# Layer 0 of a two-layer attention step: gates of heads 2 to 7 projected ahead of these heads' attention and applied with the norm; the sum of exponentials divided out in ScalarE's copy

## The chip, the core and the metric

The kernel runs on one core of one Trainium2 chip (trn2). The time is the device time of one execution in microseconds (us). In the rows of the profile PE is TensorE (PEld its weight loads), DVE is VectorE, ACT is ScalarE, POOL is GpSimd and SP is SyncE, which here only issues DMAs, in order. L694 is line 694 of the kernel before; in the changed kernel the same code stands a few lines further down.

## The reference, cut to what matters

Two layers over 1024 latent tokens and 256 context tokens of width 1024: layer 0 mixes by differential attention, layer 1 by multi-head latent attention. Each layer normalizes its input, shifts and scales it by a modulation computed from a conditioning vector, mixes, and adds the gated and normalized result. All values are fp32. Of layer 0, what bears on the change:

```python
q, k, v, gate = jnp.split(h @ w_in, ...)      # 8 heads; v and gate: 128 columns per head
def block(qb):
    s = jnp.einsum('bqhcd,bkhcd->bhcqk', qb, k) * scale
    p = jax.nn.softmax(s, axis=-1)
    w = p[:, :, 0] - lam * p[:, :, 1]
    return jnp.einsum('bhqk,bkhe->bqhe', w, v)
o = map_query_blocks(block, q)
o = rmsnorm(o, g_sub) * (1.0 - lam_init)      # over a head's 128 columns
return o.reshape(b, sq, MIX_WIDTH) * jax.nn.silu(gate)
```

The modulation is `silu(cond) @ w_ada + b_ada`, 3072 columns for each of the two layers.

## The kernel before

Tokens are held as five pairs of 128-token tiles: pairs 0 to 3 are the latent tokens, pair 4 (`CTXP`) the context. Large products are made of three matmuls each, high and low parts of both operands (`mm3`, L325 to L327).

Layer 0 runs from the start to about 965 us. A prologue ends near 60 us; then keys and queries are projected (list `P1`), to about 330 us; from there `l0_heads` runs 72 units, nine for each of the 8 heads (two for each latent pair, one for the context pair, pair order 0, 1, 4, 2, 3). Between the steps of a unit `feed(w)` advances a second stream of work by a share of the stream's estimated total. That stream is the list `P2`, whose items are joined by `chain`, which loads an item's weights while the item ahead still runs:

- `v1` to `v3` project the values, and `g0` to `g3` (in the list before: `g0` to `g2` and `y3`) the gates, of two heads each (hp = 0 to 3) for all five pairs. A pair's gate is evicted from PSUM by ACT (L487) and DVE (L488), which make twice its silu, and stored to the DRAM buffers `gdram` of the pair (L489; the trace's `g<-s`).
- `a0` to `a5` are modulation items (`ada_item`): each loads 8 pieces of `w_ada` of 128x512 fp32, 256 KB each, through the rings `wh` and `wl` of 5 buffers (L197), multiplies them (L188) with a 32-column tile, four of them writing to four different 32-row strips of one PSUM tile, copies the result out (L208) and turns it into columns (L233). Items `a6` and `a7` (`YA`) follow the last gate item.
- the last item, `gate_y_item`, projects one more pair of heads' gates, then runs `a6` and `a7`, and meanwhile steps through the list `gs` of `y_chunk(pr, kk)`; kk = 0 to 3 stands for heads 2kk and 2kk + 1. `YS` gives the counts of the stream at which a chunk may take its next step. A `y_chunk` loads 128x2x256 of the attention's result and of the gate (L750), into tiles named `kl`, `wst` or `xt`, multiplies them (DVE, L753), transposes the product by four (PE, L764), and writes the high part (ACT, L765) and the low part (DVE, L766) as operands of the out-projection. The chunks with kk = 3 are issued by `l0_heads` in the last head, and two of them after the attention (tiles `xt`).

A unit with an odd index, or of the context pair, ends with `l0_values`: the value matmuls, a copy of their sum (L688), two transposes (L691), a copy to `y` (L694). Its second half, called at the next unit's end, squares `y` times the reciprocal sum of exponentials `rz` with an accumulated sum (L698), makes the reciprocal root (DVE L250, POOL L252), multiplies by both on DVE (L702) and stores the head's 128 columns to `ydram` (L704, SP). There are 40 such posts, 5 for each head.

The PSUM tiles named `pj` come from one pool of 4 buffers, which the projections, the middle part of the scores, the transposes and the values share. The tiles `s` come from the pool `stg` with 4 buffers. SP issues every load and store named here in program order; a load that waits for a store or for a buffer holds up all behind it. The order on each engine is made by the scheduler of the language, from the program order and its own estimates.

After the attention come the out-projection of layer 0 and layer 1, to 1961 us. The change doesn't touch them.

Of the kernel before, what the change touches and what calls it, by code (L numbers as in the profile page):

```python
# [11 lines left out]
AF = mybir.ActivationFunctionType  # L12
ALU = mybir.AluOpType
# [68 lines left out]
class K:  # L82
    P1 = "k0 q0 k1 q1 k2 q2 k3 q3"
    P2 = "v1 a0 a1 v2 g0 a2 v3 a3 g1 a4 a5 g2 y3"
    YA = (6, 7)
# [589 lines left out]
    def l0_values(self, u, rz, vh, vl, feed):  # L675
# [4 lines left out]
        nch = 10 if lat else 2  # L680
        pv = self.t(c.tp, [P, 512], "pj")
        for ch in range(nch):
            g, j = ch // 4, ch % 4
            vs = ch if lat else 10 + ch
            self.mm3(pv[:, 0:256], (vh[:, vs, :], vl[:, vs, :]), (u.pth[g][:, j, :], u.ptl[g][:, j, :]),
                     ch == 0, ch == nch - 1)
# [6 lines left out]
        ss = self.t(c.st, [P, 2], "oss")  # L693
        nc.scalar.copy(y, pv[:, 256:512].rearrange("p (t d) -> p t d", t=2))  # L694
        yield

        for i in range(2):
            nc.scalar.activation(oT[:, i * P:(i + 1) * P], y[:, i, :], AF.Square,  # L698
                                 scale=rz[i], accum_out=ss[:, i:i + 1])
        r = self.rstd(c.st, ss, P, 2, tag="ors")  # L700
        for i in range(2):
            nc.vector.tensor_scalar(out=y[:, i, :], in0=y[:, i, :], scalar1=r[:, i:i + 1], scalar2=rz[i],  # L702
                                    op0=ALU.mult, op1=ALU.mult)
        nc.sync.dma_start(self.ydram[pr].rearrange("(t p) n -> p t n", p=P)[:, :, h * P:(h + 1) * P], y)  # L704
# [34 lines left out]
    def y_chunk(self, pr, kk, late=None, alt=False):  # L739

        nc, c = self.nc, self.c
        if late:
            y, g = (self.t(late, [P, 2, 256], "xt", bufs=3) for j in range(2))
        elif alt:
            y, g = (self.t(self.wp, [P, 2, 256], "wst", bufs=3) for j in range(2))
        else:
            yg = self.t(c.kst, [P, 2, 2, 256], "kl", bufs=4)
            y, g = yg[:, 0], yg[:, 1]
        for o, src in ((y, self.ydram), (g, self.gdram)):
            nc.sync.dma_start(o, src[pr].rearrange("(t p) n -> p t n", p=P)[:, :, kk * 256:(kk + 1) * 256])  # L750
        yield 1

        nc.vector.tensor_tensor(out=y, in0=y, in1=g, op=ALU.mult)  # L753
        yield 1
# [15 lines left out]
    def gate_y_item(self, hp, more):  # L770
# [7 lines left out]
        def gen(ws):  # L778
            gs = [self.y_chunk(pr, kk, alt=(3 * pr + kk) % 2) for pr in range(NPAIR) for kk in range(3)]
            at = self.YS  # L780
# [965 lines left out]
```

## Time and profile before

| | |
|---|---|
| time, median of 3 runs | 1967.2 us (1964.93 to 1968.94) |
| the profiled execution, its time | 1963.3 us |
| its span from first to last instruction | 1961.5 us |
| mean granted TensorE clock | 0.996 |
| PE busy over the span | 96% |
| DVE, ACT, POOL busy over the span | 68%, 49%, 3% |
| attention of layer 0 with its stream of projections | about 330 to 965 us |

Durations and waits are read from the profiled execution, which is 3.9 us below the median of the runs. A row of a group gives the line, the engine, the operation, the tiles written and read, the shape, the count, then the busy time in us and the mean of one in ns, then the engine's idle time ahead of these instructions and what ended it. Rows of a stretch give its start and end, its length, and for each engine the busy time and the count of instructions, then the granted clock, the mean share in which the 16 DMA engines were busy, and GB/s.

### The profile page before, as it was taken

What the parts mean: (1) busy time and instruction counts of PE and PEld (TensorE: products, weight loads), DVE (VectorE), ACT (ScalarE), POOL (GpSimd) and SP (SyncE); (2) the same over time, 40 slices, a digit from 0 to 9 for tenths busy, and PEclk for the clock granted to TensorE, in tenths of its full rate; (3) what the DMA queues carried; (4) which work ended last, traced back from release to release, by engine and by line L of the source; (5) the groups of instructions that cost most, each with busy time, mean ns of one, the idle gap of its engine ahead of it and who ended that gap; (6) DMA issues with size and microseconds to landing.
All of it is one profiled execution on the core that took longest, in us unless ns stands there. A gap on an engine that the chain in (4) does not pass through costs nothing.

```text
span 1961.5 us, 35893 instructions
## 1 busy us (share of the span) xinstructions
PE 1892.0 (96%) x13468; PEld 1712.6 (87%) x13468; DVE 1330.3 (68%) x2983; ACT 964.3 (49%) x2409; POOL 59.5 (3%) x91
## 2 busy tenths in 40 slices
PE   7999999999999999998999999999999999998998
PEld 5888888789989887987799998889899999997998
DVE  4655457788888788899537644337777877778524
ACT  4422124567666666776446633334444545456421
POOL 0000000000000000000000100000000000000000
PEclk9999999999999999999999999999999999999999
DMA  8555544444455554455525303441111111113512
GB/s 312 191 182 181 175 146 151 147 135 129 135 157 153 143 165 142 129 161 173 193 95 164 104 25 100 141 144 30 43 37 30 40 48 45 39 35 98 170 49 108
DMA packets 225006, 237.63 MB, mean 121 GB/s; under 512 B 25313, under 2 KB 192577, under 8 KB 224705
## 3 DMA queue, kind: packets, MB, share of 16 engines
q1 hardware_dynamic: 224672, 235.29, 38.7%
q8 instruction: 107, 1.75, 0.4%
q14 instruction: 67, 0.54, 0.1%
q10 hardware_dynamic: 160, 0.05, 0.0%
HBM read 160.48 MB, written 74.78 MB: 120 GB/s over the span
## 4 chain that ended last, share of the span: by engine, by line
PE 79%; DVE 11%; DMA 3%; ACT 3%; issue 2%; POOL 1%; SPq 0%; POOLq 0%; ACTq 0%; DVEq 0%
PE pj L325 16%; PE pj L327 16%; PE pj L326 16%; PE S L600 5%; PE tp L668 3%; PE tp L325 3%; PE tp L326 3%; PE tp L327 3%; DVE mA L602 2%; PE pj L668 2%; DVE ptl L671 2%; PE S L1274 1%; PE S L1276 1%; PE S L1277 1%; PE S L1275 1%
## 5 line engine op out<-in xcount | busy, mean ns | idle before, releaser
L325 PE MATMUL pj<-wh,hh 128*128 128x256 f32 (+1 forms) x1264 | 367.1, 290 | 9.1 <-DVE ptl L671 6.3
L326 PE MATMUL pj<-wl,hh 128*128 128x256 f32 (+1 forms) x1264 | 356.4, 282 | 2.3 <-DVE wl L318 2.3
L327 PE MATMUL pj<-wh,hl 128*128 128x256 f32 (+1 forms) x1264 | 356.2, 282 | 0.2
L325 PEld LDWEIGHTS pj<-wh,hh 128*128 128x128 f32 x1264 | 239.7, 190 | 14.4 <-DVE ptl L671 6.3
L326 PEld LDWEIGHTS pj<-wl,hh 128*128 128x128 f32 x1264 | 239.9, 190 | 3.5 <-DVE wl L318 2.9
L327 PEld LDWEIGHTS pj<-wh,hl 128*128 128x128 f32 x1264 | 239.4, 189 | 2.1 <-DVE hl L298 1.4
L325 PE MATMUL pj<-hh,wh 128*128 128x512 f32 (+1 forms) x512 | 188.6, 368 | 0.0
L327 PE MATMUL pj<-hh,wl 128*128 128x512 f32 (+1 forms) x512 | 188.1, 367 | 0.0
L326 PE MATMUL pj<-hl,wh 128*128 128x512 f32 (+1 forms) x512 | 188.0, 367 | 0.0
L614 ACT ACTIVATE e<-S,bias 128x1024 f32<-128x1024 f32 x128 | 143.0, 1117 | 80.9 <-DVE bias L611 80.6
L602 DVE TENSOR_REDUCE mA<-S 128x1 f32<-128x1024 f32 x128 | 155.4, 1218 | 25.4 <-PE S L600 24.9
L600 PE MATMUL S<-kl,q 128*128 128x512 f32 x512 | 148.6, 409 | 4.2 <-ACT e L614 3.6
L670 ACT CAST pth<-tp 128x512 fp32r<-128x512 f32 (+1 forms) x208 | 98.3, 511 | 79.0 <-PE tp L668 77.8
L670 ACT CAST pth<-pj 128x512 fp32r<-128x512 f32 (+1 forms) x192 | 98.0, 517 | 68.9 <-PE pj L668 66.0
L671 DVE TENSOR_TENSOR ptl<-tp,pth 128x512 fp32r<-128x512 f32 (+1 forms) x208 | 115.3, 582 | 12.3 <-ACT pth L670 11.5
L645 DVE SCALAR_TENSOR_TENSOR e<-e,cf,e 128x512 f32<-128x512 f32 (+1 forms) x192 | 117.6, 658 | 0.8
L671 DVE TENSOR_TENSOR ptl<-pj,pth 128x512 fp32r<-128x512 f32 (+1 forms) x192 | 113.2, 593 | 2.9 <-ACT pth L670 2.6
L318 DVE TENSOR_TENSOR wl<-wst,wh 128x512 fp32r<-128x512 f32 (+3 forms) x136 | 84.2, 629 | 41.2 <-ACT wh L317 40.4
L327 PEld LDWEIGHTS pj<-hh,wl 128*128 128x128 f32 x512 | 96.4, 188 | 17.2
L326 PEld LDWEIGHTS pj<-hl,wh 128*128 128x128 f32 x512 | 96.4, 188 | 16.8
L325 PEld LDWEIGHTS pj<-hh,wh 128*128 128x128 f32 x512 | 96.4, 188 | 16.8
L1291 ACT ACTIVATE e<-S,bias 128x1024 f32<-128x1024 f32 x64 | 71.5, 1118 | 76.4 <-DVE bias L1289 69.9
(316 smaller groups left out, 4941.4 us busy)
## 6 DMA issues: line engine op xcount, KB each, us to landing
q<-qsd SPq DMA_DIRECT2D x320, 64.0 KB, 2.0
wst<-in_da_w_in_dram SPq DMA_DIRECT2D x64, 256.0 KB, 3.1
kl<-ksd SPq DMA_DIRECT2D x64, 192.0 KB, 3.9
wst<-in_w_out_dram SPq DMA_DIRECT2D x48, 256.0 KB, 3.0
ast<-in_w_ada_dram SPq DMA_DIRECT2D x8, 1024.0 KB, 6.2
wh<-in_w_ada_dram SPq DMA_DIRECT2D x32, 256.0 KB, 4.3
wl<-in_w_ada_dram SPq DMA_DIRECT2D x32, 256.0 KB, 4.1
vdh<-s SPq DMA_DIRECT2D x24, 256.0 KB, 2.0
```

The lines of the kernel that those rows point to most:

```text
L318: nc.vector.tensor_tensor(out=wl, in0=st, in1=f32(wh), op=ALU.subtract)
L325: nc.tensor.matmul(out, a[0], b[0], start=first, stop=False)
L326: nc.tensor.matmul(out, a[0], b[1], start=False, stop=False)
L327: nc.tensor.matmul(out, a[1], b[0], start=False, stop=last)
L600: nc.tensor.matmul(S[:, so:so + 512], st(cc, o), kl[cc][:, so:so + 512], start=(o == 0), stop=(o == 1))
L602: nc.vector.reduce_max(out=mA[:, cc:cc + 1], in_=S, axis=AX.X)
L614: nc.scalar.activation(u.es[cc][:, 0:1024], A[cc], AF.Exp, bias=bias[:, cc:cc + 1], scale=0.125, accum_out=u.zA[:, cc:cc + 1])
L645: nc.vector.scalar_tensor_tensor(out=w[:, sl], in0=w[:, sl], scalar=cf, in1=e0[:, sl], op0=ALU.mult, op1=ALU.add)
L668: nc.tensor.transpose(tp[:, j, :], u.e[:, (c0 + j) * P:(c0 + j + 1) * P], self.ident)
L670: nc.scalar.copy(hi, tp[:, 0:cn, :])
L671: nc.vector.tensor_tensor(out=u.ptl[g][:, 0:cn, u.i * P:(u.i + 1) * P], in0=tp[:, 0:cn, :], in1=f32(hi), op=ALU.subtract)
L1291: nc.scalar.activation(e[:, 0:nm], S, AF.Exp, bias=bias, scale=sc, accum_out=Z[:, 0:1])
```

## The change

1. The list of the stream. Before, the gates of heads 0 to 5 are projected between the value items, and those of heads 6 and 7 last; after, the gates of heads 2 to 7 come right behind the values of these heads, and those of heads 0 and 1 last. The modulation items `a1` to `a5` stand in a row (before: `a0 a1`, `a2`, `a3` and `a4 a5` apart).
2. `l0_values` loads, for heads 2 to 7, the head's gate (tile `s`, 128x2x128, 128 KB, on SP) and multiplies with it where it applied `rz` before: `scalar_tensor_tensor` in place of `tensor_scalar`. Heads 0 and 1 keep a `tensor_scalar`, with one scalar.
3. `rz` is applied earlier: one copy of 128x256 (L694) becomes two activations of 128x128 with a scale, and the square (L698) has no scale any more.
4. `y_chunk` loads and multiplies the gate for kk = 0 only. The chunks of a pair are taken in the order kk = 1, 2, 0 and not 0, 1, 2.

```diff
-    P2 = "v1 a0 a1 v2 g0 a2 v3 a3 g1 a4 a5 g2 y3"
+    P2 = "v1 g1 v2 g2 a0 v3 g3 a1 a2 a3 a4 a5 y0"
...
     def l0_values(self, u, rz, vh, vl, feed):
...
+        if h > 1:
+            gt = self.t(c.stg, [P, 2, P], "s")
+            nc.sync.dma_start(gt, self.gdram[pr].rearrange("(t p) n -> p t n", p=P)[:, :, h * P:(h + 1) * P])
...
-        nc.scalar.copy(y, pv[:, 256:512].rearrange("p (t d) -> p t d", t=2))
+        for i in range(2):
+            nc.scalar.activation(y[:, i, :], pv[:, 256 + i * P:256 + (i + 1) * P], AF.Copy, scale=rz[i])
         yield
...
             nc.scalar.activation(oT[:, i * P:(i + 1) * P], y[:, i, :], AF.Square,
-                                 scale=rz[i], accum_out=ss[:, i:i + 1])
+                                 accum_out=ss[:, i:i + 1])
         r = self.rstd(c.st, ss, P, 2, tag="ors")
         for i in range(2):
-            nc.vector.tensor_scalar(out=y[:, i, :], in0=y[:, i, :], scalar1=r[:, i:i + 1], scalar2=rz[i],
-                                    op0=ALU.mult, op1=ALU.mult)
+            if h > 1:
+                nc.vector.scalar_tensor_tensor(out=y[:, i, :], in0=y[:, i, :], scalar=r[:, i:i + 1], in1=gt[:, i, :],
+                                               op0=ALU.mult, op1=ALU.mult)
+            else:
+                nc.vector.tensor_scalar(out=y[:, i, :], in0=y[:, i, :], scalar1=r[:, i:i + 1], scalar2=None,
+                                        op0=ALU.mult)
...
     def y_chunk(self, pr, kk, late=None, alt=False):
...
-            y, g = (self.t(late, [P, 2, 256], "xt", bufs=3) for j in range(2))
+            y, g = self.t(late, [P, 2, 256], "xt", bufs=3), None
         elif alt:
-            y, g = (self.t(self.wp, [P, 2, 256], "wst", bufs=3) for j in range(2))
+            y = self.t(self.wp, [P, 2, 256], "wst", bufs=3)
+            g = None if kk else self.t(self.wp, [P, 2, 256], "wst", bufs=3)
...
-        for o, src in ((y, self.ydram), (g, self.gdram)):
+        for o, src in ((y, self.ydram), (g, self.gdram))[:1 if kk else 2]:
             nc.sync.dma_start(o, src[pr].rearrange("(t p) n -> p t n", p=P)[:, :, kk * 256:(kk + 1) * 256])
         yield 1
 
-        nc.vector.tensor_tensor(out=y, in0=y, in1=g, op=ALU.mult)
+        if kk == 0:
+            nc.vector.tensor_tensor(out=y, in0=y, in1=g, op=ALU.mult)
...
-            gs = [self.y_chunk(pr, kk, alt=(3 * pr + kk) % 2) for pr in range(NPAIR) for kk in range(3)]
+            gs = [self.y_chunk(pr, kk, alt=(3 * pr + (kk + 2) % 3) % 2) for pr in range(NPAIR) for kk in (1, 2, 0)]
```

Three places show how the order of the engines' instructions moves. The first is PE, where one modulation item ends and the next begins. The last two of an item's 8 products (L188) are followed by the four small matmuls into columns (L233), and the next item's first products follow. Before, in the pair `a4 a5`; L600 and L608 are scores, L668 transposes of the exponentials:

```order
L188 MATMUL pj_9055<-wh_8807,silc_239 32x512
L188 MATMUL pj_9055<-wl_8808,silc_239 32x512
L600 MATMUL S_9142<-kl_7926,q_8989 128x512 x4
L600 MATMUL S_9155<-kl_7927,q_8989 128x512 x4
L233 MATMUL pj_9099<-sel_242,s_9097 128x2 x4
L188 MATMUL pj_9106<-wh_9078,silc_239 32x512
L188 MATMUL pj_9106<-wl_9079,silc_239 32x512
L668 MATMUL pj_9148<-identr_227,e_8917 128x128 x4
L668 MATMUL pj_9161<-identr_227,e_8917 128x128 x2
L188 MATMUL pj_9106<-wh_9080,silc_239 32x512
```

And after, one of the four such places in the row `a1` to `a5`:

```order
L188 MATMUL pj_10176<-wh_10086,silc_239 32x512
L188 MATMUL pj_10176<-wl_10087,silc_239 32x512
L233 MATMUL pj_10220<-sel_242,s_10218 128x2 x4
L600 MATMUL S_10256<-kl_9011,q_10114 128x512
L600 MATMUL S_10269<-kl_9012,q_10114 128x512
L600 MATMUL S_10256<-kl_9011,q_10114 128x512 x3
L600 MATMUL S_10269<-kl_9012,q_10114 128x512 x3
L188 MATMUL pj_10226<-wh_10199,silc_239 32x512
L188 MATMUL pj_10226<-wl_10200,silc_239 32x512
L668 MATMUL pj_10262<-identr_227,e_10025 128x128 x4
```

One item's passage to the next looks alike in both; after, there are four of them with no projection between, and the products stand in groups of other sizes along the stream.

The second place is DVE near the end of the attention, in the last head, where the chunks' multiplies (L753) stand among the weighing (L636 to L645) and the low parts of the exponentials (L671). Before:

```order
L766 SCALAR_TENSOR_TENSOR hl_2376_11436<-pj_11742,gsub_314_1097,hh_2375_11435 128x2x256
L640 SCALAR_TENSOR_TENSOR cf_11730<-Z_11549,neglam_1086,rz_11728 128x1
L753 TENSOR_TENSOR kl_11787<-kl_11787 128x512
L645 SCALAR_TENSOR_TENSOR e_11605<-e_11605,cf_11730,e_11604 128x512 x2
L645 SCALAR_TENSOR_TENSOR e_11605<-e_11605,cf_11730,e_11604 128x256
L753 TENSOR_TENSOR wst_11737<-wst_11737,wst_11738 128x512
L636 TENSOR_TENSOR Z_11672<-Z_11672,zA_11674 128x2
L753 TENSOR_TENSOR kl_11814<-kl_11814 128x512
L638 RECIPROCAL rz_11851<-Z_11672 128x2
L753 TENSOR_TENSOR kl_11905<-kl_11905 128x512
L671 TENSOR_TENSOR ptl_2459_11794<-pj_11797,pth_2456_11791 128x4x128
```

After, in the same head (L763 is the multiply's line there, L776 that of the low parts):

```order
L645 SCALAR_TENSOR_TENSOR e_11679<-e_11679,cf_11803,e_11678 128x512 x2
L645 SCALAR_TENSOR_TENSOR e_11679<-e_11679,cf_11803,e_11678 128x256
L636 TENSOR_TENSOR Z_11745<-Z_11745,zA_11747 128x2
L638 RECIPROCAL rz_11921<-Z_11745 128x2
L640 SCALAR_TENSOR_TENSOR cf_11923<-Z_11745,neglam_1086,rz_11921 128x1
L645 SCALAR_TENSOR_TENSOR e_11790<-e_11790,cf_11923,e_11789 128x512 x2
L671 TENSOR_TENSOR ptl_2483_11865<-pj_11868,pth_2480_11862 128x4x128
L645 SCALAR_TENSOR_TENSOR e_11790<-e_11790,cf_11923,e_11789 128x256
L671 TENSOR_TENSOR ptl_2484_11866<-pj_11877,pth_2481_11863 128x4x128
L763 TENSOR_TENSOR kl_11885<-kl_11885 128x512
L776 SCALAR_TENSOR_TENSOR hl_2490_11889<-pj_11890,gsub_314_1097,hh_2489_11888 128x512
```

Four multiplies stood in eleven rows; one is left, that of a chunk with kk = 0.

The third place is SP at the same stage: the loads of the chunks (L750, after: L759), the store of a fresh gate (L489), of a head's result (L704, after: L712) and the loads of `a6` and `a7` (L197). The names `y_5` and `g_10` are the context pair's `ydram` and `gdram`, `y_2` and `g_7` pair 1's. Before:

```order
L750 DMA wst_11737<-y_5_64 128x2x256
L750 DMA kl_11787<-y_1_60 128x2x256
L750 DMA kl_11787<-g_6_65 128x2x256
L197 DMA wh_11833<-in_w_ada_dram 128x512
L704 DMA y_5_64<-y_11538 128x2x128
L750 DMA wst_11738<-g_10_69 128x2x256
L197 DMA wl_11834<-in_w_ada_dram 128x512
L750 DMA kl_11814<-y_5_64 128x2x256
L750 DMA kl_11814<-g_10_69 128x2x256
L750 DMA kl_11905<-y_2_61 128x2x256
L750 DMA kl_11905<-g_7_66 128x2x256
L489 DMA g_10_69<-s_11704 128x2x256
```

After:

```order
L712 DMA y_5_64<-y_11612 128x2x128
L759 DMA kl_11885<-y_5_64 128x2x256
L759 DMA kl_11975<-y_2_61 128x2x256
L489 DMA g_10_69<-s_11777 128x2x256
L197 DMA wh_11905<-in_w_ada_dram 128x512
L197 DMA wl_11906<-in_w_ada_dram 128x512
L197 DMA wh_11907<-in_w_ada_dram 128x512
L759 DMA kl_11885<-g_10_69 128x2x256
L197 DMA wl_11908<-in_w_ada_dram 128x512
L197 DMA wh_11909<-in_w_ada_dram 128x512
```

The chunks' gate loads are gone but for kk = 0, and that of the last pair stands behind the store of the gate that it reads, with three loads of `w_ada` between.

## The prediction

> **What bounds the kernel now.** I read the page first: the head, the busy times and the shares of the chain of waits.
>
> ```profile
> span 1961.5 us, 35893 instructions
> PE 1892.0 (96%) x13468; PEld 1712.6 (87%) x13468; DVE 1330.3 (68%) x2983; ACT 964.3 (49%) x2409; POOL 59.5 (3%) x91
> PE 79%; DVE 11%; DMA 3%; ACT 3%; issue 2%; POOL 1%; SPq 0%; POOLq 0%; ACTq 0%; DVEq 0%
> ```
>
> PE is the bound. What an edit elsewhere can give back is PE's idle time, so I read next where that lies: the busy times by stretch, from the attention's body through its end to the out-projection.
>
> ```profile
> core 0: us, PE busy (x) PEld busy (x) DVE busy (x) ACT busy (x) POOL busy (x), PEclk, DMA share, GB/s
> 500.00:860.00 360.00, 353.95 (x2599) 317.10 (x2598) 309.24 (x675) 239.72 (x635) 18.47 (x23) 1.00 0.50 145
> 875.00:945.00 70.00, 61.90 (x441) 51.93 (x444) 66.67 (x143) 47.41 (x119) 4.18 (x5) 0.98 0.64 203
> 945.00:975.00 30.00, 26.74 (x217) 23.88 (x210) 13.56 (x27) 11.04 (x30) 0.69 (x1) 0.98 0.53 167
> ```
>
> In the body PE idles 6.05 of 360 us, which is 1.2 in 70, and DVE has 14% to spare. From 875 to 945 PE idles 8.1 of 70 us, and DVE is busy for 95%: there DVE is the bound. From 945 to 975, where the late chunks stand, PE idles 3.3. These three numbers are all that the attention has to give, unless PE's own work shrinks.
>
> **The chunks' multiplies.** L753 by stretch, its kinds, and the waits of that end:
>
> ```profile
> 836.00:865.00 29.00, 2.77 (x4) 1.00 0.48 140
> 865.00:960.00 95.00, 9.38 (x14) 0.98 0.57 177
> 960.00:975.00 15.00, 1.39 (x2) 1.00 0.74 237
> L753 DVE TENSOR_TENSOR xt<-xt,xt x2: 693/693/693, 967.9 to 971.9; 128x512 f32<-128x512 f32 x2
> DVE xt L753 <- DMA xt<-g: 3.9, 2, 2.8
> PE pj L764 <- DVE xt L753: 1.5, 1, 1.5
> ```
>
> Of 20 multiplies 5 stay. By the changed order of DVE 4 of them lie where 14 lay (865 to 960): 10 x 0.67 = 6.7 us less on an engine with 3.3 us free in 70. Each us that DVE is ahead there should come back to PE until PE's idle time falls to the body's 1.2, so at most 8.1 - 1.2 = 6.9. The lower end is 2: the engine still has the weighing and the low parts in a row, and PE's waits in that end are single ones of 1 to 1.5 us on different DVE results. I take **-5**, nearest to the amount of work taken off, less the part that falls between waits.
>
> The two late chunks (`xt`) lose multiply and gate load. Both sit in the out-projection's first stretch; DVE waits 3.9 us for the two gate loads and PE 1.5 for DVE. The load of `y` remains on the path, so I take only PE's own wait, **-1.5**, between 0 and the whole 3.3.
>
> **The modulation items.** L188 alone, by the stretches of the eight items, 16 records each:
>
> ```profile
> 373.00:377.00 4.00, 1.92 (x16) 0.42 (x16) 1.00 0.84 267
> 377.00:389.00 12.00, 6.29 (x16) 0.84 (x16) 1.00 0.61 194
> sum 63.00, PE 30.59 PEld 4.77; mean PE 3.82 PEld 0.60
> ```
>
> The same 8 products cost 1.92 us in one run and 6.29 in six pieces: up to four that follow each other run side by side on their strips, and a lone one takes as long as four. In the order before, the eight items fall into 2, 6, 4, 4, 2, 6, 3 and 2 such pieces, 29, so 30.59 / 29 = 1.05 us each. After, they are 2, 2, 5, 2, 4, 4, 3 and 4: 26. That is 3 x 1.05 = **-3.1** on PE itself; ends -2 and -4, as PE's order may fill such gaps otherwise.
>
> Five items stand in a row now, and they bring 40 loads of 256 KB with little projection between. What loads at full rate did to PE before:
>
> ```profile
> 376.00:382.00 6.00, 5.84 (x28) 2.93 (x26) 3.76 (x11) 3.62 (x10) 0.69 (x1) 1.00 1.00 322
> 736.00:752.00 16.00, 15.61 (x85) 7.75 (x83) 12.63 (x26) 7.95 (x23) 0.69 (x1) 1.00 0.66 206
> 924.00:938.00 14.00, 12.03 (x79) 8.23 (x80) 13.94 (x30) 8.99 (x24) 0.13 (x1) 1.00 1.00 339
> SPq L197 <- PE pj L327: 20.4, 14, 4.2
> ```
>
> In the pairs `a0 a1` (376) and `a4 a5` (736) PE lost 0.16 of 6 and 0.4 of 16 us, so the lower end is 0. One item's 2.1 MB at 322 GB/s takes 6.5 us. In the new order some 21 us of other PE work stands between the five, 5.2 for each of four gaps, so each gap could lack 1.3 us; with 3 more for the other 3.3 MB that SP moves there (10 us at that rate, most of it in the row's own 26 us), the upper end is +8. I take **+2**: nearer to the pairs, which had the same load ahead by one item, and rings of the same depth.
>
> **The copy and the square.** The rows of ACT that price the split, and who waits for the copy:
>
> ```profile
> L694 ACT COPY y<-pj 128x256 f32<-128x256 f32 x40 | 15.0, 376 | 13.3 <-PE pj L691 11.2 <-DMA y<-y 1.2 <-DVE Z L636 0.4
> L418 ACT COPY r<-pj 128x512 f32<-128x512 f32 x32 | 18.8, 586 | 130.5 <-PE pj L327 130.4
> L765 ACT ACTIVATE hh<-pj,gsub 128x512 fp32r<-128x512 f32 x20 | 13.7, 694 | 16.0 <-PE pj L764 16.0
> L698 ACT ACTIVATE oT<-y,rz 128x128 f32<-128x128 f32 x64 | 25.4, 400 | 0.6
> L1034 ACT ACTIVATE rjunk<-qa 128x384 bf16<-128x384 f32 x10 | 5.3, 526 | 0.2
>   PE pj L188: 1.5, 1
> ```
>
> Copies cost 0.82 ns a column (586 - 376 over 256), so 271 for 128; a scale from memory adds 694 - 586 = 108. Two activations make 758 against 376, +382 ns. A square without a scale of that kind, from L1034 less 256 columns, is 316 against 400, and a post has two: -168. Net 0.21 us a post, 8.6 over 40. The cover is ACT's spare time, 33% in the body and 22.6 of 70 us at the end. What is not covered is the release of the `pj` tile, 0.38 later in each post: PE waited for L694 by 1.5 us once. I take **+1**; ends 0 and 1.9, five posts' delay in the last head, where everything is late already. With the end's DVE loosened, ACT is what would be late next.
>
> **The gate within the post.** `scalar_tensor_tensor` with the gate takes the place of `tensor_scalar`, 60 times:
>
> ```profile
> L702 DVE TENSOR_SCALAR y<-y,ors,rz x64: 336/343/350, 348.8 to 958.7; 128x128 f32<-128x128 f32 x64
> L645 DVE SCALAR_TENSOR_TENSOR e<-e,cf,e 128x512 f32<-128x512 f32 x128 | 91.7, 747 | 0.8
> L632 DVE SCALAR_TENSOR_TENSOR e<-e,cfx 128x256 f32<-128x256 f32 x16 | 7.3, 480 | 0.1
> ```
>
> The operation takes 747 ns at 512 and 480 at 256, 1.04 a column, so 346 at 128 against 343: **0**. The most is 0.9 us in the last stretch, were each 70 ns dearer; below zero nothing speaks for it.
>
> The Trainium skill speaks against this edit: "VectorE: DVE Perf Modes", section "The perf-mode tier table (the rule you actually need)", gives fp32 `tensor_scalar` in SBUF twice the rate, and an operation with two tensor inputs the single one. By it 128 columns would take some 67 ns more (an estimate from that page's durations), 4 us over the 60, of them 0.9 in the last stretch, and the sum below would be -4.7. The trace doesn't bear it out: by the rows of L645 and L632 the two cost the same at this size.
>
> The 30 loads of 128 KB that fetch the gate stand on SP:
>
> ```profile
> y<-y SPq DMA_DIRECT2D x40, 128.0 KB, 1.9
> wst<-g SPq DMA_DIRECT2D x7, 256.0 KB, 4.3
> g<-s SPq DMA_DIRECT2D x20, 256.0 KB, 2.2
> ```
>
> They are issued ahead of the value matmuls and needed after the norm, some 10 us of work later, so a 4.3 us load is covered in the body: **0**. The 15 gate loads of the chunks that go are 3.9 MB, and so are the 30 added, so traffic is level. The upper end is +3: in head 6 the load of a post stands behind 16 loads of `w_ada`, and late gates hold the single `y` buffer, whose store had the copy wait 1.2 us in the row of L694.
>
> Chunks with kk = 0 load a gate that was just projected. For the last pair, 2.2 us for the store and 4.3 for the load make 6.5, beside some 8.7 us of other DVE work that the new order puts between, but with three loads of 256 KB ahead in the queue. **+1**, ends 0 and +4 (2 us for those three loads and 2 more if the store waits as well).
>
> **The sum.** -5 - 1.5 - 3.1 + 2 + 1 + 0 + 0 + 1 = -5.6 us, against the profiled execution's 1963.3: 1957.7. That execution lies 3.9 below the runs' median of 1967.2, so the forecast for the median is **1961.6**, 0.29% faster. About 0.2%, 3.9 us, is what a measurement of this kernel can tell from no change. With every low end the sum is -14, with every high one about +14.
>
> **Rivals.** *No change: the end is bound by more than DVE.* In 924 to 938 the DMA engines are full too (1.00, 339 GB/s, the loads of `a6`), and both stay. If the last posts' chain through SP and POOL and these loads set the pace, the DVE relief yields only 2, and the late chunks 0, since `y` of the last head must still be stored and loaded: -2 - 3.1 + 2 + 1 + 1 = -1.1, 1966.1. For it: the single waits there come from many sides. Against: DVE was busy 13.94 of those 14 us.
>
> *Slower: SP stands still in the row of five.* SP waits for a ring buffer with everything behind it, queries and gates included; before, that was 20.4 us in 14 waits, all hidden. If one batch of 16 loads, 4.2 MB, 12.7 us at 330 GB/s, delays a query load or a post's gate fully once, that is +12.7 in place of +2: -5.6 + 10.7 = +5.1, 1972.3. It decides from a stall of 11.5 us on, which moves the sum past +3.9. Against: the pairs before lost 0.4 us at most, and queries are loaded three units ahead.
>
> *A larger gain: all idle time at the end returns, and nothing is paid elsewhere:* -6.9 - 3.3 - 3.1 + 1 for the copy = -12.3, 1954.9. For it: 95% against the body's 86% on DVE.
>
> **How the numbers follow.** Forecast 0.47 (own range 1957 to 1965), no change 0.28, slower 0.14, the larger gain 0.11. Faster than 0.2% means 1963.3 or less: 0.38 of the forecast's chance, all of the larger gain and 0.05 of the no-change case, 0.54. Within: 0.09 + 0.20 + 0.03 of the slower case, 0.32. Slower: 0.03 + 0.11 = 0.14. The range 1951 to 1971 takes in both bounds of the forecast's large terms and leaves out the deep end of the stall and of the gain.
>
> **What the changed profile would show.** In the last 70 us of the attention DVE below 90% busy and PE's idle time near 3 us; in the next 30 no wait for a gate load; L188 near 27.5 us in all; the two activations near 380 ns and the multiply with the gate near 345; in the row of five, PE's idle time below 3 us, with DMA share near 1. The forecast is wrong if PE's idle time at the end stays at 8 with DVE relieved, if a wait for `w_ada`, a query or a gate of several us shows in head 6, or if PE's waits for the copies' tile grow past a few us.

## The result, and the profile after

The changed kernel takes 1992.8 us (median of four runs, 1990.9 to 1994.9) against 1966.9 for the kernel before: ratio 1.0129, 95% interval 1.0115 to 1.0143. It is 26 us slower, where 5.6 us less were forecast. The profiled execution took 1990.9. The head of its page, its busy times and the shares of its chain of waits:

```profile
span 1989.1 us, 35955 instructions
PE 1901.3 (96%) x13468; PEld 1719.0 (86%) x13468; DVE 1322.9 (67%) x2968; ACT 964.6 (48%) x2449; POOL 58.8 (3%) x91
PE 77%; DVE 13%; ACT 3%; DMA 3%; issue 2%; POOL 1%; SPq 0%; ACTq 0%; POOLq 0%; DVEq 0%
```

The span grew by 27.6 us. PE ran as many matmuls, was busy 9.3 us longer, and idled 87.8 us where it had idled 69.5, 18.3 more. Where the idle time came shows in the busy times by stage. From 500 us on the stages are cut at the same points of the work in both kernels: at the first scores of head 6, of head 7, at the last scores, and some 55 us later, in the out-projection. First before, then after:

```profile
core 0: us, PE busy (x) PEld busy (x) DVE busy (x) ACT busy (x) POOL busy (x), PEclk, DMA share, GB/s
330.00:500.00 170.00, 160.09 (x1158) 141.80 (x1157) 140.62 (x307) 109.12 (x285) 7.93 (x10) 1.00 0.47 137
500.00:780.00 280.00, 274.13 (x1996) 242.41 (x1995) 237.90 (x523) 184.30 (x487) 14.65 (x18) 1.00 0.51 148
780.00:854.00 74.00, 73.89 (x565) 69.66 (x563) 65.68 (x144) 50.60 (x134) 3.82 (x5) 1.00 0.51 144
854.00:927.00 73.00, 67.91 (x486) 60.31 (x487) 69.19 (x146) 53.24 (x139) 4.18 (x5) 1.00 0.50 149
927.00:980.00 53.00, 46.66 (x361) 39.46 (x360) 32.74 (x67) 24.96 (x62) 1.38 (x2) 0.97 0.63 206
```

```profile
330.00:500.00 170.00, 161.74 (x1210) 150.11 (x1210) 143.28 (x314) 112.37 (x305) 7.57 (x10) 1.00 0.41 118
500.00:771.00 271.00, 257.60 (x1920) 237.10 (x1919) 230.94 (x502) 180.72 (x496) 15.03 (x18) 1.00 0.49 140
771.00:869.00 98.00, 89.14 (x576) 66.40 (x575) 70.04 (x154) 50.87 (x140) 3.45 (x5) 0.97 0.63 189
869.00:945.00 76.00, 69.46 (x504) 62.37 (x504) 66.42 (x140) 52.61 (x141) 3.81 (x5) 1.00 0.53 158
945.00:1000.00 55.00, 46.67 (x310) 36.95 (x309) 25.81 (x54) 20.81 (x54) 1.38 (x2) 0.88 0.46 146
```

PE's idle time in the body (500 us to head 6) went from 5.9 to 13.4 us, in head 6 from 0.1 to 8.9, in head 7 from 5.1 to 6.5, behind it from 6.3 to 8.3; from 330 to 500 us it is 9.9 and 8.3. The body's 7.5 us are nearly as large a loss as head 6's 8.8, and no term of the prediction stands for them. Head 6, where the five modulation items now stand in a row, takes 98 us and not 74 (part of that is the items' own work, which left the heads ahead of it). In head 7 DVE is relieved as forecast, 87% busy and not 95%, and PE idles there no less than before: in this stage the relief bought nothing.

The other 9.3 us are the clock, the granted share of TensorE's full speed. These rows are stretches of the changed kernel; the number behind the busy times is the granted clock:

```profile
816.00:820.00 4.00, 2.20 (x18) 0.45 (x17) 3.25 (x13) 2.92 (x14) 0.69 (x1) 1.00 0.17 46
820.00:828.00 8.00, 6.38 (x20) 4.38 (x20) 4.90 (x10) 0.00 (x0) 0.00 (x0) 0.57 0.91 300
956.00:960.00 4.00, 2.12 (x19) 1.88 (x18) 2.88 (x6) 2.39 (x7) 0.69 (x1) 1.00 0.63 207
960.00:968.00 8.00, 6.54 (x28) 3.53 (x28) 4.21 (x11) 2.44 (x4) 0.00 (x0) 0.57 0.27 88
978.00:982.00 4.00, 0.94 (x7) 0.46 (x5) 2.17 (x5) 3.28 (x11) 0.69 (x1) 0.90 0.19 65
982.00:988.00 6.00, 5.92 (x27) 5.92 (x28) 0.02 (x1) 0.00 (x0) 0.00 (x0) 0.50 0.66 188
```

Behind three pauses of PE the clock stands at half for some 7 us: 0.43 x 8 twice, and 0.1 x 4 with 0.5 x 6, make 3.4 us lost in each of three places. The profiled execution of the kernel before has one such place in the attention, behind a wait of 1.5 us for the copy that two of the three pauses also wait for (below):

```profile
PE pj L233 <- DVE s L208: 1.5, 1, 1.5
942.00:944.00 2.00, 1.70 (x11) 1.73 (x12) 2.00 (x5) 0.00 (x0) 0.40 (x1) 0.72 0.41 136
944.00:948.00 4.00, 4.00 (x26) 1.52 (x25) 2.50 (x7) 1.91 (x4) 0.00 (x0) 0.71 0.22 64
```

0.28 x 2 and 0.29 x 4 make 1.7 us. Part of the difference is luck of the execution: this one had a mean clock of 0.996, where the middle one of 83 executions of the kernel before, beside the experiments, had 0.993. What PE waited for in the row of five, and in the end:

```profile
PE pj L233 <- DVE s L208: 3.2, 1, 3.2
PE pj L233 <- DVE m L610: 1.4, 1, 1.4
PE S L600 <- ACT e L614: 1.4, 1, 1.4
PE pj L188 <- DMA wh<-in_w_ada_dram: 1.3, 1, 1.3
PE pj L233 <- DVE s L208: 3.3, 1, 3.3
PE xt L923 <- ACT gp L928: 2.3, 1, 2.3
```

The first four rows are from 790 to 850 us, the last two from 945 to 1000. In both stages the longest is a modulation item's column step (L233) that waits for DVE's copy of its products out of PSUM (L208). In the body of the kernel before no such wait was over 0.6 us. The order of PE tells why. Where I showed it ahead of the prediction I called the passages alike in both kernels; they are not. Before, eight scores stand between an item's last products and its column step; after, in the place shown, the column step follows at once. In the traces 4 to 50 matmuls stand there in the kernel before; in the row of five it is 4, 10, 0, 2 and 0, and behind the two zeros PE stands idle for 3.2 and 1.4 us, while the copy is still behind other work on DVE.

In the end 18 matmuls stand there in both kernels, and the copy is later. DVE's only wait between 957 and 962 us, and the chain of waits (start, length, what):

```profile
DVE hl L776 <- ACT hh L775: 1.0, 2, 0.5
958.82 0.60 ACT hh L775
...
960.11 0.60 DVE y L707 x2
960.71 0.61 DVE s L208
...
961.46 1.84 PE pj L233 x8
```

The products are there at 956.0, and the copy starts at 960.6. Ahead of it in DVE's queue stand, among others, a chunk's multiply (L763), two chunks' low parts (L776), which wait 1.0 us for their high parts on ACT (L775), and a post's multiply with the gate (L707). PE stands at L233 until that is through, and starts again at half clock.

### The profile page after: what moved, and what is told of

The parts are those of the page before. It is cut to its first block, busy times and chain, and to the rows that moved or that the text cites. A ratio compares the mean times of both kernels' runs of the same rounds, so it can differ in the third digit from the quotient of the medians.

```text
span 1989.1 us, 35955 instructions
## 1 busy us (share of the span) xinstructions
PE 1901.3 (96%) x13468; PEld 1719.0 (86%) x13468; DVE 1322.9 (67%) x2968; ACT 964.6 (48%) x2449; POOL 58.8 (3%) x91
## 4 chain that ended last, share of the span: by engine, by line
PE 77%; DVE 13%; ACT 3%; DMA 3%; issue 2%; POOL 1%; SPq 0%; ACTq 0%; POOLq 0%; DVEq 0%
PE pj L325 16%; PE pj L327 15%; PE pj L326 15%; PE S L600 4%; PE tp L668 3%; DVE mA L602 3%; PE tp L325 3%; PE tp L326 3%; PE tp L327 3%; DVE ptl L671 2%; PE pj L668 2%; PE S L1286 1%; PE S L1287 1%; PE S L1284 1%; PE S L1285 1%
## 5 line engine op out<-in xcount | busy, mean ns | idle before, releaser
L614 ACT ACTIVATE e<-S,bias 128x1024 f32<-128x1024 f32 x128 | 143.0, 1117 | 94.2 <-DVE bias L611 94.2
L600 PE MATMUL S<-kl,q 128*128 128x512 f32 x512 | 149.4, 412 | 7.0 <-ACT e L614 7.0
L671 DVE TENSOR_TENSOR ptl<-tp,pth 128x512 fp32r<-128x512 f32 (+1 forms) x208 | 115.3, 582 | 12.3 <-ACT pth L670 11.5
L645 DVE SCALAR_TENSOR_TENSOR e<-e,cf,e 128x512 f32<-128x512 f32 (+1 forms) x192 | 118.8, 658 | 1.3
L671 DVE TENSOR_TENSOR ptl<-pj,pth 128x512 fp32r<-128x512 f32 (+1 forms) x192 | 113.3, 593 | 4.8 <-ACT pth L670 4.6
L317 ACT CAST wh<-wst 128x512 fp32r<-128x512 f32 (+3 forms) x136 | 77.1, 574 | 71.8 <-PE pj L326 21.0
L668 PE MATMUL pj<-identr,e 128*128 128x128 f32 x640 | 106.2, 275 | 5.0 <-DVE e L645 1.9
```

The costliest lines, as they stand in the source:

```text
L317: nc.scalar.copy(wh, st)
L600: nc.tensor.matmul(S[:, so:so + 512], st(cc, o), kl[cc][:, so:so + 512], start=(o == 0), stop=(o == 1))
L614: nc.scalar.activation(u.es[cc][:, 0:1024], A[cc], AF.Exp, bias=bias[:, cc:cc + 1], scale=0.125, accum_out=u.zA[:, cc:cc + 1])
L645: nc.vector.scalar_tensor_tensor(out=w[:, sl], in0=w[:, sl], scalar=cf, in1=e0[:, sl], op0=ALU.mult, op1=ALU.add)
L668: nc.tensor.transpose(tp[:, j, :], u.e[:, (c0 + j) * P:(c0 + j + 1) * P], self.ident)
L671: nc.vector.tensor_tensor(out=u.ptl[g][:, 0:cn, u.i * P:(u.i + 1) * P], in0=tp[:, 0:cn, :], in1=f32(hi), op=ALU.subtract)
```

## The experiments

All runs are against the kernel before, run beside them; a ratio of 1.0129 is the changed kernel's. 0.1% is 2 us.

**List alone.** `P2` and the order of the chunks as changed, all else as before.

> The kernel before with the changed kernel's list of items and its order of chunks alone: posts, copies and all twenty multiplies of the chunks as before. Theory 'row' (the five modulation items in a row in head 6 leave PE without projection work, 22 us; the fresh gate of the last chunk costs the rest): 1988 to 2000 us. Theory 'post' (the dearer copies and the gate loads of the posts cost the time): 1965 to 1975. Within 'row', if the ten multiplies taken off DVE near the end are worth the 5 us I forecast, it is 5 us or more above the changed kernel (1998); if they are hidden, level with it (1993).

1983.1 us, ratio 1.0074 (1.0059 to 1.0089). The list alone costs 14.6 us. Its head 6:

```profile
771.00:869.00 98.00, 89.62 (x585) 66.46 (x584) 71.32 (x157) 52.24 (x138) 3.81 (x5) 0.98 0.61 190
```

PE idles 8.4 us there, as in the changed kernel: that loss belongs to the list, not to gates or copies. So does most of the body's: from 500 to 771 us PE idles 12.6 us here, against 13.4 in the changed kernel. The time lies between the two expected ranges, 11 us below the changed kernel's though all multiplies are back. So the multiplies near the end are hidden, or worth less than the copies and the posts cost; the run with the copy whole, below, takes the two apart.

**Split copy alone.**

```diff
-        nc.scalar.copy(y, pv[:, 256:512].rearrange("p (t d) -> p t d", t=2))
+        for i in range(2):
+            nc.scalar.activation(y[:, i, :], pv[:, 256 + i * P:256 + (i + 1) * P], AF.Copy, scale=rz[i])
...
```

> The kernel before with one edit: the copy split into two activations with the scale, the square and the norm's multiply without it. Theory 'row': 1967 to 1969, the 1 us I priced. Theory 'post': 1975 or more.

1991.2 us, ratio 1.0112 (1.0095 to 1.0129): 22.7 us from the edit that I had priced at 1. Its durations were as worked out; what waits for it was not:

```profile
L695 ACT ACTIVATE y<-pj,rz 128x128 f32<-128x128 f32 x64 | 20.1, 367 | 11.8 <-PE pj L691 11.7
L699 ACT ACTIVATE oT<-y 128x128 f32<-128x128 f32 x80 | 25.1, 322 | 0.0
PE pj L608 <- ACT y L695: 1.5, 1, 1.5
PE pj L188 <- ACT y L695: 1.4, 1, 1.4
```

Two activations of 367 ns and two squares of 322 (forecast: 379 and 316). But PE's waits for the copy, here from 370 to 780 us, are 3 us: they don't explain 22. Two other things grew. From the first scores of head 2 to the last scores PE waits 12.9 us for the low parts of the exponentials (DVE, L671), where it waited 5.9 in the kernel before. And the four executions had a mean clock of 0.989, against 0.993 of the kernel before beside them, which is some 8 of the 22.7 us.

**One load for five items.** `a2` to `a5` return `a1`'s tiles in place of loading.

> The changed kernel, in which the items a2 to a5 use the weights that a1 loaded: 32 loads of 256 KB are left out (and with them the right modulation of layer 1), the matmuls stay. Theory 'loads' (the row of five is bound by 10.5 MB of loads): 15 to 20 us of the 26 come back, 1973 to 1978. Theory 'thin stream' (PE has no independent work beside the attention's own chain of scores, maximum, exponentials and transposes while the five items run, whatever their loads do): under 6 us come back, 1987 or more.

1983.4 us, ratio 1.0075 (1.0060 to 1.0090): 11 us came back, between the two expectations. Head 6:

```profile
773.00:866.00 93.00, 86.55 (x578) 69.07 (x577) 70.32 (x155) 51.66 (x143) 3.44 (x5) 0.94 0.44 126
```

PE still idles 6.5 of the 8.9 us without the loads. Another part of the gain is PE's own: the items' matmuls take 26 us and not 30, since they run in fewer pieces (rows below, under the modulation matmuls). The longest wait, 2.9 us, is again a column step's for its copy. Neither theory alone holds; most of the pauses don't come from the loads.

**The five items in the first projection.** `P1 = "k0 a1 q0 a2 k1 a3 q1 a4 k2 a5 q2 k3 q3"`, without them in `P2`.

> The changed kernel with a1 to a5 moved out of head 6 into the projection of keys and queries, one behind each of the first five projections, where PE is busy throughout. Theory 'row', in either form: the loss in head 6 goes and some 15 us of matmuls move with the items, so 1968 to 1976. Theory 'post': 1988 or more.

2023.0 us, ratio 1.0272 (1.0257 to 1.0288), the worst of all. That is in the range given to 'post', but not for its reason: the wait of PE between 60 and 400 us shows a miss of mine.

```profile
PE pj L188 <- DMA wh<-in_w_ada_dram: 18.8, 7, 5.7
```

The items' loads land after PE has come to them, and PE, which is busy nearly throughout there before, stands for each. The clock falls with it, to 0.94 over the first 330 us. So the run decides nothing between the two theories.

The 22 us, with 3 us of waits for the copy, suggested that the order that the scheduler lays around an edit decides. Several of the next runs test it.

**Another order for nothing.** `AC = 240.0` in place of 215 (the planner's ns for a modulation matmul) in the kernel before.

> The kernel before with one number of the planner changed: a modulation matmul is put at 240 ns and not 215, so that the stream beside the attention is paced a little differently. No instruction is added, taken away or changed; the scheduler lays some 120 places of PE's order anew. Theory 'order' (the split copy alone cost 23 us mainly because the order around it was laid anew, and this order was a good one): 1975 to 1990 us. Theory 'ScalarE's time' (the split copy cost it through ACT's 0.2 to 0.4 us a post): 1966 to 1972.

1964.4 us, ratio 0.9975 (0.9963 to 0.9987). Some 120 places of PE's order differ, and it is 0.25% faster, a little below both expectations: this new order by itself costs nothing.

**Split without the scale.**

```diff
-        nc.scalar.copy(y, pv[:, 256:512].rearrange("p (t d) -> p t d", t=2))
+        for i in range(2):
+            nc.scalar.copy(y[:, i, :], pv[:, 256 + i * P:256 + (i + 1) * P])
```

> The kernel before with the copy in two halves of 128 columns, without the scale, and square and multiply as before: the instruction is added, but only 166 ns a post where the split with the scale added 382. Theory 'ScalarE's time': 40% of that loss or less, 1971 to 1978. Theory 'order': not tied to the 166 ns, anywhere between 1968 and 1992, and its PE waits differ from those of the split with the scale in place and kind.

1966.6 us, ratio 0.9983 (0.9971 to 0.9994).

```profile
L695 ACT COPY y<-pj 128x128 f32<-128x128 f32 x80 | 17.4, 272 | 14.8 <-PE pj L691 11.1 <-DMA y<-y 3.4
```

Two copies of 272 ns, 168 ns more a post, cost nothing at all, which is below both expectations. So the added instruction is free, and the loss hangs on the scaled form or on the order that came with it. The durations speak for the order: with their squares, and the reading of the sums behind each, ACT's instructions of a post take 1.78 us here and 1.79 in the split with the scale, and DVE's two multiplies 0.69 and 0.57. PE's order differs from that of the kernel before in some 50 places here, and in some 140 there.

**The change with the copy whole.** The changed kernel with `rz` back in the square's scale, and the root's reciprocal multiplied by it in two small DVE operations for heads 2 to 7.

> The changed kernel with the copy in one piece and the reciprocal sums kept where they were: in the square's scale, and for heads 2 to 7 multiplied into the root's reciprocal by two small DVE operations a post. So the change without its ACT part. Theory 'ScalarE's time': 15 to 20 us come back, 1972 to 1978. Theory 'order': the row of five and the late gate remain, 1980 to 1992.

1990.0 us, ratio 1.0092 (1.0071 to 1.0113): the split copy's part of the change is 0.37%, 7 us (with an uncertainty of 0.25%), with two small DVE operations a post in its place. Against the list alone, at 1.0074, this run has the gates in the posts and ten multiplies less near the end, and it is no faster. The small operations, 0.21 us each and ten in a head, give back some 2 of the 6.7 us that the multiplies took. So the multiplies near the end are hidden.

**An old gate at the end.** The chunks with kk = 0 load columns 256 to 511 of the gate.

> The changed kernel in which the chunks of heads 0 and 1 load another gate, that of heads 2 and 3, which was stored long before: same loads and multiplies, no wait for a fresh store (and a wrong product for two heads). If the fresh gate sets the 10 us that were lost in the attention's last 30 us: 1982 to 1986. If other waits there do (the modulation items and the clock that falls in PE's pauses): 1989 or more.

1988.9 us, ratio 1.0088 (1.0065 to 1.0111): 0.41%, 8 us back (with an uncertainty of 0.27%), against the before beside it that was 2 us slower than in the first measurement. The stage behind the last scores, cut as above:

```profile
949.00:1004.00 55.00, 48.93 (x352) 39.73 (x351) 28.21 (x59) 24.62 (x63) 1.38 (x2) 0.94 0.51 159
```

PE idles 6.1 us there and not 8.3, and the clock is 0.94 and not 0.88; its wait for the copy at the column step is 2.0 us and not 3.3. That the fresh gate did this is not shown: in the trace of the changed kernel DVE waits for a chunk's gate only once, 2.2 us at the start of head 7, and not at all behind the last scores; here such waits are 2.6 us.

**Split copy, other order.** The split copy alone, with `AC = 240.0`.

> The kernel before with the split copy and its scale (the edit that cost 23 us alone) and with the planner's number for a modulation matmul at 240 as in the run that laid the order anew for nothing. Theory 'ScalarE's time' (the two scaled activations cost 22 us in themselves): 1985 to 1993. Theory 'order' (that run's order was a bad one, and the edit itself is cheap): 1975 or less.

1972.7 us, ratio 1.0028 (1.0017 to 1.0040), against 0.9975 for the same number without the split: 0.53%, 10 us. By this pair the edit, with the order that it brings, costs 10 us, and the rest of the first run's 22.7 belongs to that order. PE's waits for the low parts (L671), from head 2 to the last scores, double here too, from 5.5 us to 11.4; in the split without the scale they are 5.4.

**The row spread wider.** The changed kernel with `AC = 600.0`.

> The changed kernel with a modulation matmul put at 600 ns in the planner, so that the five items in a row are spread over six units of the attention and not two and a half; still no projection between them. Theory 'loads' (PE waits in the row because 10.5 MB come in too short a time): 10 us or more come back, 1982 or less. Theory 'thin stream' (PE stands still because the attention's own chains have nothing beside them, for as long as the row lasts): 1988 to 2000.

1979.7 us, ratio 1.0066 (1.0045 to 1.0087), 12 us back, inside the range that I gave to the loads. But the rows say something else:

```profile
330.00:500.00 170.00, 167.12 (x1258) 155.94 (x1258) 143.96 (x316) 113.00 (x306) 6.91 (x10) 1.00 0.43 124
783.00:860.00 77.00, 70.49 (x490) 58.12 (x489) 65.32 (x148) 48.77 (x136) 4.19 (x5) 0.98 0.66 189
```

In head 6, where three of the five items now stand, PE still idles 6.5 us. What fell is the idle time between 330 and 500 us, from 8.3 to 2.9, long before the first modulation item: I take it that a planner that puts the items higher feeds the projections faster from the start, and that they fill PE there. So this run doesn't tell loads from a thin stream. The kernel before idles 9.9 us in the same stretch, so what came back here was not lost by the change.

**The row in the kernel before.** `P2 = "v1 a0 v2 g0 v3 g1 a1 a2 a3 a4 a5 g2 y3"`.

> The kernel before with its own gates and posts, but with a1 to a5 in a row ahead of g2 (list v1 a0 v2 g0 v3 g1 a1 a2 a3 a4 a5 g2 y3). If a row of five items costs by itself: 1979 to 1993. If it costs only beside the changed gates and posts: 1966 to 1973.

1972.1 us, ratio 1.0020 (1.0009 to 1.0032). The stretch of its row, and that of the changed kernel's:

```profile
704.00:758.00 54.00, 49.67 (x258) 25.94 (x258) 31.94 (x71) 20.23 (x55) 1.38 (x2) 0.94 0.75 229
```

```profile
794.00:849.00 55.00, 47.00 (x261) 27.35 (x261) 35.04 (x80) 21.65 (x61) 2.07 (x3) 0.94 0.72 225
```

Some 260 matmuls in 55 us, at the same clock and load traffic, with 4.3 and 8.0 us of idle PE. The time lies in the range for a row that costs only beside the changed gates and posts, but the list alone, without these, lost 14.6 us. This list costs 4 us in all; its row loses about as much as that in idle PE, 3.8 of the 4.3 us at column steps (L233), and 3 us more by the clock.

**The last items' copy on ScalarE.**

```diff
-            self.nc.vector.tensor_copy(m, pt)
+            if (l, ch) in ((1, 4), (1, 5)):
+                self.nc.scalar.copy(m, pt)
+            else:
+                self.nc.vector.tensor_copy(m, pt)
```

> The changed kernel in which ScalarE and not VectorE copies the results of a6 and a7 out of PSUM. In the changed kernel PE waited 3.3 us for a6's copy, which stood on DVE behind a post's multiply with the gate, and the clock fell after it. If this queue is what the end lost: 6 to 9 us come back, 1984 to 1987. If the wait only moves to another instruction: 1990 or more.

1983.4 us, ratio 1.0083 (1.0065 to 1.0101): 9 us back, as expected of the queue on DVE, and a little more. PE's wait of 3.3 us at the column step is now (same step, three lines down):

```profile
PE pj L236 <- ACT s L209: 0.7, 1, 0.7
```

**Two more orders of the changed kernel, one of the kernel before.** `AC` at 240 and 190, nothing else.

> The changed kernel with the planner's number for a modulation matmul at 240 and not 215, nothing else. Theory 'change' (its 26 us belong to the edits: the row of five in head 6, the split copy, the late end): within 5 us of the changed kernel, 1988 to 1998. Theory 'order' (a good part is the accident of which instruction stands behind which in the queues): anywhere, and more than 6 us off in at least one of the two such runs.

1995.9 us, ratio 1.0144 (1.0118 to 1.0171).

> The changed kernel with that number at 190. As for the run with 240: theory 'change' 1988 to 1998, theory 'order' more than 6 us off in at least one of the two.

1992.8 us, ratio 1.0117 (1.0092 to 1.0143).

> The kernel before with that number at 190: the third order of the kernel before. Theory 'change': within 5 us of before, 1963 to 1972, as the order with 240 was. Theory 'order': off by 6 us or more.

1969.0 us, ratio 1.0002 (0.9992 to 1.0012). Three orders of the changed kernel lie at 1.0117 to 1.0144, three of the kernel before at 0.9975 to 1.0002. The loss belongs to the edits, and not to one unlucky order.

**Mended.** The changed kernel with `AC = 600.0` and all modulation results copied by ScalarE.

> The changed kernel with two mends in one: the modulation matmuls put at 600 in the planner (12 us came back by that alone) and the results of all modulation items copied out of PSUM by ScalarE and not VectorE (9 us came back by that for the last two alone). If the two losses are separate: 1966 to 1974. If the second mend only helped by another order at the end: 1976 to 1984. If it beats the kernel before: under 1964.

1970.6 us, ratio 1.0013 (0.9999 to 1.0027): 1.16% came back, where the two mends gave 0.63 and 0.46 alone. They add.

**Mended, copy whole.** The same with the post's copy in one piece, as in the run above that kept it whole.

> The mended changed kernel (600 in the planner, modulation results copied by ScalarE) with the post's copy in one piece again and two small DVE operations a post in its place, so the list and the gates of the change without its split copy. The split copy cost 7 us in the changed kernel: 1961 to 1966 if that adds to the mends; 1968 to 1973 if the mends already hide it. Under 1966 it beats the kernel before.

1961.5 us, ratio 0.9958 (0.9944 to 0.9973): faster than both kernels. The split copy is worth 0.55%, 11 us, here. Between 330 and 500 us, around the row of five, and behind the last scores, which come at 929 us here:

```profile
330.00:500.00 170.00, 168.00 (x1279) 157.90 (x1278) 147.39 (x319) 115.67 (x305) 7.36 (x10) 1.00 0.43 123
760.00:860.00 100.00, 90.67 (x642) 75.09 (x643) 85.56 (x208) 66.64 (x176) 5.87 (x7) 1.00 0.67 188
929.00:984.00 55.00, 50.96 (x419) 47.03 (x417) 27.10 (x61) 25.22 (x68) 1.69 (x2) 1.00 0.38 117
```

The row of five still leaves PE idle, 9.3 us in the 100 around it; the longest wait there is one of 3.3 us for a query load. Of the gain over the changed kernel, part lies ahead of the row, 2.0 us of idle time where the changed kernel had 8.3 and the kernel before 9.9, and part in the end, 4.0 us of idle time where the changed kernel had 8.3, at full clock and not at 0.88.

**The mend without the change.** The kernel before with `AC = 240.0` and ScalarE's copies.

> The kernel before with 240 in the planner (0.25% faster than before by that alone) and the modulation results copied out of PSUM by ScalarE. If the copies wait behind posts on DVE there too: 1958 to 1962; if not, level with the run at 240 alone, 1963 to 1966.

1969.5 us, ratio 0.9996 (0.9985 to 1.0007): no gain, even a loss against 0.9975, and outside both expected ranges. In the kernel before these copies cost nothing that ScalarE would give back.

## Why the prediction was wrong, point by point

- *The multiplies (-5): wrong.* DVE was relieved as worked out, and nothing came back: the change with the copy whole (1.0092), without ten of them near the end, was no faster than the list alone (1.0074), with all. The step that failed is "each us that DVE is ahead there should come back to PE". An engine that is 95% busy need not be what PE waits for; PE's waits there were single ones on different results, which I had noted and not followed.
- *The late chunks (-1.5):* their waits for gate loads (3.9 us on DVE, 1.5 on PE behind it) went, and a larger one of PE in the same stage, 2.3 us for ACT (L923), took their place.
- *The modulation matmuls (-3.1): not there.* The eight items took 30.6 us before. After, and in the run with one load for five, L188 from 600 to 1000 us:

```profile
600.00:1000.00 400.00, 30.36 (x128) 4.72 (x128) 0.97 0.53 158
```

```profile
600.00:1000.00 400.00, 25.82 (x128) 4.30 (x128) 0.97 0.48 140
```

  The pieces counted in the order are not all that sets the time. Two of the changed kernel's items, `a1` and `a7`:

```profile
794.00:800.00 6.00, 3.58 (x16) 0.66 (x16) 1.00 1.11 360
964.00:973.00 9.00, 5.26 (x16) 0.67 (x16) 0.81 0.31 103
```

  The first, in two pieces, took 3.58 us and not 1.92, at full clock beside loads at 360 GB/s; the second, in four, 5.26 and not 4.2, at a clock of 0.81. That a load that arrived late split the first is my reading.
- *The row of five (+2, at most 8): the term most undersized.* The list costs 14.6 us alone, and in head 6 8.4 us of idle PE and a fall of the clock. I asked what the loads would delay; what failed is that step. Of the 8.9 us of idle PE in the changed kernel's head 6, 4.6 are at two column steps that wait for DVE with no matmul between them and their item's products, and 1.3 at a load. My 0.16 and 0.4 us came from pairs of items in which scores or projections stood there. And the list costs idle time in the body too, some 7 us more than before, which I had put at nothing; in the changed kernel PE waits there 6.5 us for the low parts (before 3.1) and 4.3 for ACT's exponentials (before 0.4). Why these grew was not tested.
- *The split copy (+1, at most 1.9): 7 to 11 us* (0.37%, 0.53% and 0.55% in three pairs of runs). The durations were right to some 3%. "The cover is ACT's spare time" is the step that failed. A longer chain of the post is not the reason either: with its shorter squares and multiplies the split with the scale keeps ACT as long, and DVE less long, than the split without, which cost nothing. What the runs show is that PE's waits for the low parts of the exponentials doubled in both orders, and that the clock fell more often. Whether the scaled copy itself holds up those low parts, or the order that the scheduler lays when the copy needs `rz`, stays open.
- *`scalar_tensor_tensor` with the gate (0): right, but the comparison behind it was not.*

```profile
L710 DVE TENSOR_SCALAR y<-y,ors x20: 280/285/289, 349.5 to 489.7; 128x128 f32<-128x128 f32 x20
L707 DVE SCALAR_TENSOR_TENSOR y<-y,ors,s 128x128 f32<-128x128 f32 x60 | 18.9, 348 | 12.0 <-POOL ors L252 11.9
s<-g SPq DMA_DIRECT2D x30, 128.0 KB, 2.6
```

  348 ns against 343. By the Trainium skill ("VectorE: DVE Perf Modes", "The perf-mode tier table (the rule you actually need)") the second tensor would make it some 67 ns dearer, an estimate from that page's durations. The trace agrees where like stands beside like: with one scalar, in heads 0 and 1, the `tensor_scalar` took 285 ns, 63 less. The 343 ns that I compared with had a second scalar, which cost 58; the edit took that out as it put the tensor in, and the two are near equal by chance. The gate's loads took 2.6 us, and PE waited for none: also 0, as taken.
- *The fresh gate (+1, at most 4):* no wait for it shows behind the last scores. 8 us came back with an old gate, but the trace doesn't show by what, and the uncertainty is two thirds of it.
- *The clock: missing from the sum.* Pauses of 3.2, 3.3 and 2.3 us each cost another 3.4 us behind them. The Trainium skill ("TensorE: Matmul & The Clock Gate", "What's actually happening") says that the clock halves after an idle window of about 3.4 us and returns after as much busy time. The halved clock is what these rows show; but the kernel before lost its 1.7 us after a wait of only 1.5 us, so by these rows a pause need not fill such a window. The clock records of the 20 traces show what counts: in each of them all falls begin on one grid of 3.41 us, and each of the 84 windows of this grid, past the start and at full clock, in which PE was busy for less than 42% was followed by a fall, as were 14 of some 11,000 in which it was busy for over 62%. So the same pause can cost or not: one of 2.8 us at 529 us in the changed kernel cost nothing, and one of 2.9 at the same step, in the list alone, 1.7 us more.

The rival of the slower side had the right place and sign, and its price of 12.7 lies near the 14.6 of the list by chance: in head 6 of the changed kernel PE waited for no query load. Of the changed kernel's 1.29%, the list makes 0.74, the split copy 0.37, and what is left, 0.18, is within the uncertainty of the three. The 0.41 and 0.46 of the two runs that changed the end are not a fourth part: the parts above already make up the whole, so they lie within list and copy.

Three things stay open: how the split copy costs its 7 to 11 us; why PE idles nearly twice as long in the row of head 6 as in that of the kernel before; and what a planner's number of 600 would do to the kernel before, which was not tried. That kernel idles 9.9 us between 330 and 500 us, where 600 left the changed one 2.9, so the 0.42% of the fastest run can't be put down to the gates.

## What to carry to other kernels

An engine's spare time is no cover for an instruction in a chain, and an engine's load is no proof that the bound engine waits for it: follow the waits. Where the bound engine takes its work in order, count what stands between a step that makes a result for another engine and the step that takes it back; with nothing there it waits for that engine's whole queue, and it pays again where the clock falls. When an edit's loss looks too large, lay the order anew with a planner's number, with and without the edit: two more runs told 10 us that came with the edit from 12 of one order.

## What the runs showed that was not expected

- A fall of the granted clock comes in steps, 3.4 or 6.8 us at half speed in the attention (1.7 or 3.4 us lost), behind pauses of 1.5 to 3.3 us. It goes with most of the scatter between executions: of 83 of the kernel before, the four with a mean clock of 0.990 or less took 1973.2 to 1975.3 us, the eight with 0.995 or more 1961.9 to 1966.8.
- A scale from memory makes ACT's copy of 128x128 367 ns, against 272 without; the square without it takes 322 ns, against 400. A second scalar makes DVE's multiply of 128x128 343 ns, against 285 with one.
- Orders of PE's 13,468 matmuls that differ in some 120 places move the kernel before by 0.25% and no more, but the split copy alone by 0.84%.
